# Down projection of a decoder layer by Strassen's seven products

## The chip, the cores and the metric

The kernel runs on one NeuronCore of a Trainium2 chip. The metric is the device time of one execution in microseconds; the profile's times count from the first recorded instruction. The engines are named as in the profile: PE (TensorE, with PEld for its weight loads), DVE (VectorE), ACT (ScalarE), POOL (GpSimd) and SP (SyncE, which here only issues transfers).

## The reference

One decoder layer over 512 tokens of 1024 channels: a mixer (mLSTM heads and a convolution group), and then a feed-forward part of 2816 hidden channels. The change is in the latter:

```python
u = rms_norm(x, ffn_pre_g[l]) * (1.0 + sc2) + sh2
up = causal_dwconv(u @ ffn_up[l], ffn_conv_w[l], ffn_conv_b[l])
a, gt = jnp.split(up, 2, axis=-1)
f = (jax.nn.silu(gt) * a) @ ffn_down[l]
x = x + g2 * rms_norm(f, ffn_post_g[l])
```

All arrays are float32.

## The kernel before, in words

Matmuls run in three passes on rounded values: each operand is split into a high part (a rounded copy by ACT, L182) and a low part (the rest, by a subtraction on POOL or DVE, L183), and `mm3` (L198) adds high x high, high x low and low x high in PSUM. `w_load` (L186) loads up to 2048 columns of weights with one transfer on SP's queue into one of two `raws` buffers and splits them into pieces of 512 columns; a pool of 20 tiles holds the split pieces, so about two and a half loads are ahead of PE.

The up projection goes over 22 blocks i of 128 hidden channels. Block i has a half `a` and a half `gt`, 8 x 3 matmuls each with all 512 tokens as the moving side. ACT and DVE then make the causal convolution of three taps (`conv3`, L967: ACT the bias and the last tap from PSUM, DVE the two others), ACT the SiLU of the gate, DVE the product, and ACT and DVE its high and low part; both stay in SBUF in `slots` (44 tiles of 128x512) for all 22 blocks, in the layout channels x tokens.

The down projection adds up 22 row blocks k into eight PSUM banks, four token tiles of 128 by two halves of 512 output columns. Each bank gets 3 matmuls per row block. The first 18 row blocks go row block by row block over all banks; the last four are gone through one token tile after the other, so that the tail of a tile (multiplication by g2, RMS norm, addition of x, store; L1037 to L1049) runs while PE works on the next.

SP and PE execute in the order of the code. For ACT, DVE and POOL a scheduler orders the instructions when the program is built; on the chip each engine then goes strictly through its list, and an instruction that waits holds all behind it. SP's transfers too are issued in one list.

Of the kernel before, what the change touches and what calls it, by code (L numbers as in the profile page):

```python
# [17 lines left out]
P = 128  # L18
# [36 lines left out]
def decoder_layer(ctx, tc, w_glu0, x, c, adaT, vecs, w_glu, w_qko, w_v0, w_v, w_out, w_up, w_down, out):  # L55
# [32 lines left out]
    def slot(name, dt=F32):  # L88
        return slots.tile([P, T], dt, tag="t", name=name)
# [4 lines left out]
    def atbank(name):  # L94
        return psum.tile([P, T], F32, tag="at", bufs=2, name=name)
# [102 lines left out]
    def mm3(ps, a, b, start, stop):  # L198

        PE.matmul(ps, a[0], b[0], start=start, stop=False)  # L200
        PE.matmul(ps, a[0], b[1], start=False, stop=False)  # L201
        PE.matmul(ps, a[1], b[0], start=False, stop=stop)  # L202
# [772 lines left out]
    f = []  # L975
    for i in range(NF):
        if i < NE:
            pa, pg = early[i]
        else:
            pieces = w_load(w_up[i], f"wup{i}")  # L980
            if i in (4, 8, 12, 16):
                ada_block(38 + i // 2, last_lo[0])
                ada_block(39 + i // 2, last_lo[0])
# [16 lines left out]
        V.tensor_tensor(out=a, in0=a, in1=g, op=ALU.mult)  # L1000
        if i < 2:
            hl = vpool.tile([P, 2 * T + 8], F32R, tag="vh", name=f"fhl{i}")
            hi, lo = hl[:, :T], hl[:, T : 2 * T]
        else:
            hi, lo = slot(f"fh{i}", F32R), slot(f"fl{i}", F32R)
        S.activation(hi, a, AF.Copy)
        V.tensor_tensor(out=lo, in0=a, in1=hi.bitcast(F32), op=ALU.subtract)
        f.append((hi, lo))


    KD = 18
    fsq = const.tile([P, 2 * NT], F32, name="fsq")
    banks = [[atbank(f"dn{tt}_{hf}") if tt == 0 else cvbank(f"dn{tt}_{hf}") if tt == 1 else mmbank(f"dn{tt}_{hf}")
              for hf in range(2)] for tt in range(NT)]
    wd = {}

    def down_rows(k):

        if k % 2 == 0:
            pieces = w_load(w_down[k // 2], f"wd{k}")  # L1020
            wd[k], wd[k + 1] = pieces[:2], pieces[2:]
        return wd[k]

    def down_mm(k, tt):
        for hf in range(2):
            mm3(banks[tt][hf], (f[k][0][:, tok(tt)], f[k][1][:, tok(tt)]), wd[k][hf], k == 0, k == NF - 1)

    for k in range(KD):
        down_rows(k)
        for tt in range(NT):  # L1030
            down_mm(k, tt)
    for k in range(KD, NF):
        down_rows(k)
    for tt in range(NT):
        for k in range(KD, NF):
            down_mm(k, tt)
# [80 lines left out]
```

## Time and profile before

| what | value |
|---|---|
| median of 3 runs | 800.17 us (799.45 to 800.42) |
| span of the profiled execution, first to last instruction | 795.9 us |
| granted clock of TensorE over the span | 0.995 of full speed |
| up projection, first matmul to first matmul of the down projection | 424.7 to 668.3 us |
| down projection, first to last matmul | 668.3 to 788.1 us |
| HBM read, written | 102.08 MB, 4.21 MB |
| weight transfers of 1024 KB in the down projection | 11, landing 4.8 us after issue |

The executions of the runs agree within 0.1%. The profile gives, by engine, the busy time and what ended the idle time before an instruction. The chain of waits follows the last instruction back through what released each step. In the view in order of time, the columns are start, duration, engine, line, operation, tiles and shape.

### The profile page before, as it was taken

How to read it: one execution, taken by the hardware profiler on the slowest of the kernel's cores; microseconds unless marked ns; L12 is line 12 of the kernel's file. 1: busy time of each engine (PE TensorE's matmuls, PEld its weight loads, DVE VectorE, ACT ScalarE, POOL GpSimd, SP SyncE). 2: the span in 40 equal slices, each digit the busy share in tenths (PEclk: the TensorE clock that was granted, in tenths of full speed). 3: DMA queues.
4: the chain of work that ended last, by engine and by line, in shares of the span. 5: the costliest groups of instructions: out<-in, count | busy, mean ns of one | idle time of the engine just before them, and what ended most of it. 6: DMA issues, size and time to landing. Idle time of an engine off the chain costs nothing.

```text
span 795.9 us, 10370 instructions
## 1 busy us (share of the span) xinstructions
PE 781.6 (98%) x3786; PEld 652.2 (82%) x3786; DVE 474.5 (60%) x748; ACT 380.1 (48%) x709; POOL 436.5 (55%) x351
## 2 busy tenths in 40 slices
PE   7999999999999999999999999999999999999996
PEld 5888897777888888888889988888888888888885
DVE  6769999999996435547958794455444453000014
ACT  6684548758474454561345454444444444212212
POOL 4789759869598433442841474444454444444420
PEclk9999999999999999999999999999999999999998
DMA  8963214122037231426854652222222222222205
GB/s 326 347 243 133 81 61 153 54 105 107 28 94 250 80 133 55 159 106 235 320 187 157 218 180 106 106 75 84 106 106 106 105 90 97 107 105 106 80 0 186
DMA packets 24887, 106.97 MB, mean 134 GB/s; under 512 B 2914, under 2 KB 2946, under 8 KB 17412
## 3 DMA queue, kind: packets, MB, share of 16 engines
q1 hardware_dynamic: 16740, 83.22, 29.3%
q10 hardware_dynamic: 8096, 23.08, 8.2%
q8 instruction: 30, 0.49, 0.3%
q14 instruction: 21, 0.17, 0.1%
HBM read 102.08 MB, written 4.21 MB: 134 GB/s over the span
## 4 chain that ended last, share of the span: by engine, by line
PE 90%; DVE 5%; ACT 1%; DMA 1%; issue 1%; DVEq 0%; POOL 0%; SPq 0%; POOLq 0%; ACTq 0%
PE up L201 10%; PE up L200 10%; PE up L202 10%; PE dn L202 5%; PE dn L200 5%; PE dn L201 5%; PE qko L200 4%; PE qko L201 4%; PE qko L202 4%; PE glu L345 4%; DVE cv L716 3%; PE glu L200 2%; PE glu L201 2%; PE glu L202 2%; PE s L514 2%; PE mixa L202 2%
## 5 line engine op out<-in xcount | busy, mean ns | idle before, releaser
L716 DVE SCALAR_TENSOR_TENSOR cv<-gt,cvw,cv 128x502 f32<-128x502 f32 (+24 forms) x200 | 134.4, 725 | 1.9 <-ACT cv L704 1.3
L1043 DVE TENSOR_TENSOR fo<-dn,g2r 128x512 f32<-128x512 f32 x8 | 5.5, 692 | 100.3 <-PE dn L202 100.3
L712 POOL TENSOR_TENSOR cs<-cs,cs 128x510 f32<-128x510 f32 (+3 forms) x32 | 42.8, 1341 | 3.6 <-ACT cs L710 3.6
L183 POOL TENSOR_TENSOR wup_1024l<-wup,wup_1024h 128x512 fp32r<-128x512 f32 x20 | 27.0, 1348 | 31.8 <-ACT wup_1024h L182 31.7
L183 POOL TENSOR_TENSOR wup_1536l<-wup,wup_1536h 128x512 fp32r<-128x512 f32 x20 | 27.0, 1352 | 29.1 <-ACT wup_1536h L182 29.0
L183 POOL TENSOR_TENSOR wup_512l<-wup,wup_512h 128x512 fp32r<-128x512 f32 x20 | 26.8, 1338 | 23.4 <-ACT wup_512h L182 23.4
L183 POOL TENSOR_TENSOR wup_0l<-wup,wup_0h 128x512 fp32r<-128x512 f32 x20 | 27.2, 1358 | 20.8 <-ACT wup_0h L182 20.8
L201 PE MATMUL up<-u2l,wup_0h 128*128 128x512 f32 (+1 forms) x100 | 36.5, 365 | 0.2 <-DVE u2l L885 0.2
L200 PE MATMUL up<-u2h,wup_0h 128*128 128x512 f32 (+1 forms) x100 | 36.5, 365 | 0.0
L200 PE MATMUL up<-u2h,wup_1024h 128*128 128x512 f32 (+1 forms) x100 | 36.4, 364 | 0.0
L202 PE MATMUL up<-u2h,wup_0l 128*128 128x512 f32 (+1 forms) x100 | 36.4, 364 | 0.0
L200 PE MATMUL up<-u2h,wup_512h 128*128 128x512 f32 (+1 forms) x100 | 36.4, 364 | 0.0
L201 PE MATMUL up<-u2l,wup_512h 128*128 128x512 f32 (+1 forms) x100 | 36.4, 364 | 0.0
L202 PE MATMUL up<-u2h,wup_512l 128*128 128x512 f32 (+1 forms) x100 | 36.4, 364 | 0.0
L200 PE MATMUL up<-u2h,wup_1536h 128*128 128x512 f32 (+1 forms) x100 | 36.4, 364 | 0.0
L201 PE MATMUL up<-u2l,wup_1536h 128*128 128x512 f32 (+1 forms) x100 | 36.4, 364 | 0.0
L202 PE MATMUL up<-u2h,wup_1536l 128*128 128x512 f32 (+1 forms) x100 | 36.4, 364 | 0.0
L202 PE MATMUL up<-u2h,wup_1024l 128*128 128x512 f32 (+1 forms) x100 | 36.4, 364 | 0.0
L201 PE MATMUL up<-u2l,wup_1024h 128*128 128x512 f32 (+1 forms) x100 | 36.3, 363 | 0.0
L167 DVE SCALAR_TENSOR_TENSOR junk<-ada,cb 128x1024 bf16<-128x1024 f32 x20 | 32.6, 1631 | 6.3 <-DMA ada<-in_adaT 6.2
L183 POOL TENSOR_TENSOR wqko_1024l<-wqko,wqko_1024h 128x512 fp32r<-128x512 f32 x12 | 16.6, 1380 | 25.8 <-PE v L201 15.1
L183 POOL TENSOR_TENSOR wd_1024l<-wd,wd_1024h 128x512 fp32r<-128x512 f32 x11 | 14.3, 1296 | 29.8 <-ACT wd_1024h L182 29.8
(727 smaller groups left out, 2617.0 us busy)
## 6 DMA issues: line engine op xcount, KB each, us to landing
wup<-in_w_up SPq DMA_DIRECT2D x22, 1024.0 KB, 4.8
wqko<-in_w_qko SPq DMA_DIRECT2D x12, 1024.0 KB, 4.7
wd<-in_w_down SPq DMA_DIRECT2D x11, 1024.0 KB, 4.8
ada<-in_adaT ACTq DMA_DIRECT2D x20, 512.0 KB, 5.6
ada<-in_adaT SPq DMA_DIRECT2D x16, 512.0 KB, 7.6
wo<-in_w_out SPq DMA_DIRECT2D x8, 1024.0 KB, 4.7
spare<-in_adaT ACTq DMA_DIRECT2D x12, 512.0 KB, 8.4
wglu<-in_w_glu SPq DMA_DIRECT2D x5, 1024.0 KB, 8.3
```

The costliest lines, as they stand in the source:

```text
L167: t = V.scalar_tensor_tensor(out=junk, in0=r, scalar=1.0, in1=cb, op0=ALU.mult, op1=ALU.mult, accum_out=mod[:, i : i + 1])
L183: (eng or G).tensor_tensor(out=lo[:, :n], in0=src, in1=hi[:, :n].bitcast(F32), op=ALU.subtract)
L200: PE.matmul(ps, a[0], b[0], start=start, stop=False)
L201: PE.matmul(ps, a[0], b[1], start=False, stop=False)
L202: PE.matmul(ps, a[1], b[0], start=False, stop=stop)
L345: PE.matmul(ps, blk(wk, i)[a], u[k][b], start=k == 0 and p == 0, stop=k == KT - 1 and p == 1)
L514: PE.matmul(sp[:, :n], ks[d][:, cc * P : (cc + 1) * P], qs[d][:, cc * P :], start=d == 0, stop=d == 1)
L712: G.tensor_tensor(out=side[:, d:], in0=side[:, d:], in1=t[:, d:], op=ALU.add)
L716: last_tap = V.scalar_tensor_tensor(out=cp[:, d:], in0=cvx[j][:, : T - d], scalar=w(CK - 1 - d), in1=cp[:, d:], op0=ALU.mult, op1=ALU.add)
L1043: V.tensor_tensor(out=m, in0=banks[tt][hf], in1=g2r[hf], op=ALU.mult)
```

## The change

The hidden channels of the first 18 row blocks are taken as nine pairs, the 512 tokens as two halves, and the 1024 output columns as two halves, so that a pair gives a product of 2x2 blocks: A11, A12 (first token half, even and odd row block), A21, A22 and B11 to B22 (the weights). Strassen's identity in Winograd's form makes the four output blocks from seven products instead of eight:

- left sides: x = (A11, A12); y with A21 + A22 and that minus A11; q with A11 - A21 and A12 minus the second half of y; and A22;
- right sides: B11, B21, B22 as they are, and four sums t1 to t4 of the B's;
- products p1, p2, p6, p5, p7, p3, p4 in this order, each over all nine pairs, 6 matmuls per pair, in one or two of the output blocks' banks. Partial results are copied from PSUM (`keep`, ACT) and added to other banks (`put`, DVE).

The sums of the weights are made during the up projection, at blocks 3, 4, 6, 8, 10, 11, 13, 15 and 17: SP loads four pieces of 256 KB of a pair into `slots`, DVE and POOL make two subtractions each, and SP stores the four sums in DRAM two blocks later. For the activations, POOL makes the four half sums of each pair; x and y are split and stay in SBUF, q and A22 go to DRAM (`spill`) and come back in the down projection (`back`: load, high part by ACT, low part by POOL). The weights of the products come in transfers of three pairs (768 KB) and are split with the low part on DVE and POOL in turn. The last four row blocks are computed as before. Nothing of the result is left out.

The core of the diff:

```diff
-    def mm3(ps, a, b, start, stop):
-
-        PE.matmul(ps, a[0], b[0], start=start, stop=False)
-        PE.matmul(ps, a[0], b[1], start=False, stop=False)
-        PE.matmul(ps, a[1], b[0], start=False, stop=stop)
+    def mm3(ps, a, b, start, stop, again=False):
+
+        for i, (l, r) in enumerate(((a[0], b[0]), (a[0], b[1]), (a[1], b[0]))):
+            PE.matmul(ps, l, r, start=start and i == 0, stop=stop and i == 2, skip_group_check=again)
...
+    JP = 9
+    NP = 2 * JP
+    GJ = 3
+    AT = [NE + 7 * j // 4 for j in range(JP)]
+    spill = {q: dram.tile([P, JP * T], F32, tag=f"spill{q}", name=f"spill{q}") for q in ("t1", "t2", "t3", "t4", "s34", "a22")}
+    sums = {}
+
+    def weight_load(j):
+        sums[j] = [slot(f"b{j}_{q}") for q in range(4)]
+        for q, t in enumerate(sums[j]):
+            nc.sync.dma_start(t, w_down[j][:, q * T : (q + 1) * T])
+
+    def weight_sums(j):
+
+        b11, b12, b21, b22 = sums[j]
+        V.tensor_tensor(out=b11, in0=b12, in1=b11, op=ALU.subtract)
+        G.tensor_tensor(out=b12, in0=b22, in1=b12, op=ALU.subtract)
+        V.tensor_tensor(out=b22, in0=b22, in1=b11, op=ALU.subtract)
+        G.tensor_tensor(out=b21, in0=b21, in1=b22, op=ALU.subtract)
+
+    def weight_store(j):
+        for q, t in zip(("t1", "t3", "t4", "t2"), sums.pop(j)):
+            nc.sync.dma_start(spill[q][:, j * T : (j + 1) * T], t)
...
+            if i in AT:
+                weight_load(AT.index(i))
+            if i - 2 in AT:
+                weight_store(AT.index(i - 2))
+            if i % 2 == 0 and 4 <= i < 4 + NP:
+                j = (i - 4) // 2
+                x_, r_, q_ = rest[j]
+                nc.sync.dma_start(spill["s34"][:, j * T : (j + 1) * T], q_)
+                nc.sync.dma_start(spill["a22"][:, j * HT : (j + 1) * HT], r_[:, HT:])
...
+            if i % 2 == 0:
+                x_, r_ = slot(f"fx{i}"), slot(f"fr{i}")
+            cs = slice(i % 2 * HT, (i % 2 + 1) * HT)
+            V.tensor_tensor(out=x_[:, cs], in0=a[:, :HT], in1=g[:, :HT], op=ALU.mult)
+            V.tensor_tensor(out=r_[:, cs], in0=a[:, HT:], in1=g[:, HT:], op=ALU.mult)
+            if i % 2:
+                y_, q_ = slot(f"fy{i}"), slot(f"fq{i}")
+                G.tensor_tensor(out=y_[:, :HT], in0=r_[:, :HT], in1=r_[:, HT:], op=ALU.add)
+                G.tensor_tensor(out=y_[:, HT:], in0=y_[:, :HT], in1=x_[:, :HT], op=ALU.subtract)
+                G.tensor_tensor(out=q_[:, :HT], in0=x_[:, :HT], in1=r_[:, :HT], op=ALU.subtract)
+                G.tensor_tensor(out=q_[:, HT:], in0=x_[:, HT:], in1=y_[:, HT:], op=ALU.subtract)
+                af.append(split_f(x_, f"fx{i}", i == 1))
+                asum.append(split_f(y_, f"fy{i}", i == 1))
+                rest.append((x_, r_, q_))
+        if i in AT:
+            weight_sums(AT.index(i))
...
+    def product(weights, left, th, hf, start, name):
+
+        for a in range(0, JP, GJ):
+            r = raws.tile([P, 2048], F32, tag="raw", name=f"{name}_{a}")
+            view = weights(a)
+            nc.sync.dma_start(r[:, : GJ * T].rearrange("p (j n) -> p j n", j=GJ), view)
+            for n in range(GJ):
+                j = a + n
+                turn[0] += 1
+                w = w_split(r[:, n * T : (n + 1) * T], f"{name}_{j}", eng=V if turn[0] % 2 else G)
+                hi, lo, off = left(j)
+                for q in range(2):
+                    ts = slice(off + q * P, off + (q + 1) * P)
+                    mm3(banks[2 * th + q][hf], (hi[:, ts], lo[:, ts]), w, start and j == 0, j == JP - 1, True)
+
+    def plain(q):
+        return lambda a: w_down[a : a + GJ, :, q * T : (q + 1) * T].rearrange("j p n -> p j n")
+
+    def summed(q):
+        return lambda a: spill[q][:, a * T : (a + GJ) * T].rearrange("p (j n) -> p j n", j=GJ)
+
+    def keep(th, hf, name):
+        out = [cvtile(f"{name}{q}") for q in range(2)]
+        for q, t in enumerate(out):
+            S.activation(t, banks[2 * th + q][hf], AF.Copy)
+        return out
+
+    def put(kept, th, hf):
...
+    def back(q, a, n, name):
+        t = slot(f"{name}r")
+        nc.sync.dma_start(t[:, :n], spill[q][:, a : a + n])
+        hi, lo = slot(f"{name}h", F32R), slot(f"{name}l", F32R)
+        S.activation(hi[:, :n], t[:, :n], AF.Copy)
+        G.tensor_tensor(out=lo[:, :n], in0=t[:, :n], in1=hi[:, :n].bitcast(F32), op=ALU.subtract)
+        return hi, lo
+
+    product(plain(0), lambda j: (*af[j], 0), 1, 1, True, "p1")
+    p1 = keep(1, 1, "kp1")
+    product(plain(2), lambda j: (*af[j], HT), 0, 0, True, "p2")
+    put(p1, 0, 0)
+    product(summed("t2"), lambda j: (*asum[j], HT), 1, 1, False, "p6")
+    u2 = keep(1, 1, "ku2")
+    s34 = [back("s34", j * T, T, f"s34_{j}") for j in range(JP)]
+    product(summed("t1"), lambda j: (*asum[j], 0), 0, 1, True, "p5")
+    p5 = keep(0, 1, "kp5")
+    product(summed("t3"), lambda j: (*s34[j], 0), 1, 1, False, "p7")
+    u3 = keep(1, 1, "ku3")
+    put(p5, 1, 1)
+    a22 = [back("a22", a * HT, min(T, (JP - a) * HT), f"a22_{a}") for a in range(0, JP, 2)]
+    product(plain(3), lambda j: (*s34[j], HT), 0, 1, False, "p3")
+    put(u2, 0, 1)
+    product(summed("t4"), lambda j: (*a22[j // 2], j % 2 * HT), 1, 0, True, "p4")
+    put(u3, 1, 0)
```

What follows shows how the lists of the engines change. A name like `wup11_512h` is the high part (`l`: the low part) of the piece of `wup11` from column 512 on; `fa10c` and `fg10c` are the two halves of block 10 in the convolution, L970/L969 is its step on ACT, L999/L1043 the SiLU. First ACT's list around block 10, before:

```order
L182 ACTIVATE wup12_1536h_5336<-wup12_5322 128x512
L970 ACTIVATE fa10c_5226<-up10_0_5176,vec_108 128x512
L182 ACTIVATE wup13_0h_5414<-wup13_5412 128x512
L182 ACTIVATE wup13_512h_5418<-wup13_5412 128x512
L970 ACTIVATE fg10c_5230<-up10_1_5201,vec_108 128x512
L182 ACTIVATE wup13_1024h_5422<-wup13_5412 128x512
L999 ACTIVATE fg10c_5230<-fg10c_5230 128x512
L1006 ACTIVATE fh10_5236<-fa10c_5226 128x512
L182 ACTIVATE wup13_1536h_5426<-wup13_5412 128x512
L970 ACTIVATE fa11c_5308<-up11_0_5258,vec_108 128x512
```

And the same place after the change (`fy9` is the sum y of the pair of blocks 8 and 9; L1007 makes its high part):

```order
L1007 ACTIVATE fx9h_5272<-fx8_5179 128x512
L969 ACTIVATE fa10c_5362<-up10_0_5312,vec_108 128x512
L1007 ACTIVATE fy9h_5276<-fy9_5266 128x512
L969 ACTIVATE fg10c_5366<-up10_1_5337,vec_108 128x512
L1043 ACTIVATE fg10c_5366<-fg10c_5366 128x512
L182 ACTIVATE wup11_0h_5381<-wup11_5379 128x512
L182 ACTIVATE wup11_512h_5385<-wup11_5379 128x512
L182 ACTIVATE wup11_1024h_5389<-wup11_5379 128x512
L182 ACTIVATE wup11_1536h_5393<-wup11_5379 128x512
L182 ACTIVATE wup12_0h_5486<-wup12_5484 128x512
```

Between the two steps of block 10 stood the splits of wup13; now no split stands there, and that of wup11 follows behind the SiLU of block 10. POOL's list at this place held only splits, `wup12_1536l`, `wup13_0l` and so on; now it is this (`fy9`, `fq9` are half sums of the pair 8, 9; `b4` are the weights of the fifth pair):

```order
L1055 TENSOR_TENSOR fy9_5266<-fr8_5180 128x256
L1057 TENSOR_TENSOR fq9_5267<-fx8_5179,fr8_5180 128x256
L1056 TENSOR_TENSOR fy9_5266<-fy9_5266,fx8_5179 128x256
L1058 TENSOR_TENSOR fq9_5267<-fx8_5179,fy9_5266 128x256
L990 TENSOR_TENSOR b4_1_5299<-b4_3_5301,b4_1_5299 128x512
L992 TENSOR_TENSOR b4_2_5300<-b4_2_5300,b4_3_5301 128x512
L183 TENSOR_TENSOR wup11_0l_5382<-wup11_5379,wup11_0h_5381 128x512
L183 TENSOR_TENSOR wup11_512l_5386<-wup11_5379,wup11_512h_5385 128x512
```

The low part of wup11 stands behind six operations of the change. Two of them take in what DVE makes here:

```order
L971 SCALAR_TENSOR_TENSOR fa10c_5362<-up10_0_5312,vec_108,fa10c_5362 128x511
L971 SCALAR_TENSOR_TENSOR fa10c_5362<-up10_0_5312,vec_108,fa10c_5362 128x510
L1008 TENSOR_TENSOR fy9l_5277<-fy9_5266,fy9h_5276 128x512
L989 TENSOR_TENSOR b4_0_5298<-b4_1_5299,b4_0_5298 128x512
L971 SCALAR_TENSOR_TENSOR fg10c_5366<-up10_1_5337,vec_108,fg10c_5366 128x511
L971 SCALAR_TENSOR_TENSOR fg10c_5366<-up10_1_5337,vec_108,fg10c_5366 128x510
L991 TENSOR_TENSOR b4_3_5301<-b4_3_5301,b4_0_5298 128x512
```

The sums `b4_0` and `b4_3` stand between and behind the taps of block 10. The last place is ACT at the change from product p6 to p5 in the down projection (`ku2` copies the banks of p6 out of PSUM, `s34` is what was spilled as q):

```order
L1108 ACTIVATE s34_5h_6765<-s34_5r_6763 128x512
L1096 ACTIVATE ku20_6729<-dn2_1_6427 128x512
L1096 ACTIVATE ku21_6730<-dn3_1_6428 128x512
L1108 ACTIVATE s34_6h_6771<-s34_6r_6769 128x512
L1108 ACTIVATE s34_7h_6777<-s34_7r_6775 128x512
L1108 ACTIVATE s34_8h_6783<-s34_8r_6781 128x512
L182 ACTIVATE p5_0h_6789<-p5_0_6787 128x512
```

Before, this list held only splits of weights (`wd4_1024h`, `wd4_1536h`, `wd6_0h` and so on) at that place; now p5's first split follows the two copies. POOL there:

```order
L1109 TENSOR_TENSOR s34_5l_6766<-s34_5r_6763,s34_5h_6765 128x512
L1109 TENSOR_TENSOR s34_6l_6772<-s34_6r_6769,s34_6h_6771 128x512
L1109 TENSOR_TENSOR s34_7l_6778<-s34_7r_6775,s34_7h_6777 128x512
L1109 TENSOR_TENSOR s34_8l_6784<-s34_8r_6781,s34_8h_6783 128x512
L183 TENSOR_TENSOR p5_0l_6790<-p5_0_6787,p5_0h_6789 128x512
```

More of the change, by code (lines that the diff above doesn't have):

```diff
@@ L1013, in decoder_layer @@
-    banks = [[atbank(f"dn{tt}_{hf}") if tt == 0 else cvbank(f"dn{tt}_{hf}") if tt == 1 else mmbank(f"dn{tt}_{hf}")
-              for hf in range(2)] for tt in range(NT)]
-    wd = {}
[L1017 to L1026, printed above, removed]
@@ new lines, in plain @@
+    def plain(q):
[8 more added lines that the diff above has]
+    def put(kept, th, hf):
+        for q, t in enumerate(kept):
+            ps = banks[2 * th + q][hf]
+            V.tensor_tensor(out=ps, in0=ps, in1=t, op=ALU.add)
```

42 lines of the change are left out of this document (24 added, 18 removed).

## Prediction

> **What bounds the kernel now.** I read the page first (busy shares, the 40 slices, the chain of waits), then the windows of the two stages that the change touches, then the order of time inside one block of the up projection.
>
> ```profile
> span 795.9 us, 10370 instructions
> ...
> PE 781.6 (98%) x3786; PEld 652.2 (82%) x3786; DVE 474.5 (60%) x748; ACT 380.1 (48%) x709; POOL 436.5 (55%) x351
> ...
> PE 90%; DVE 5%; ACT 1%; DMA 1%; issue 1%; DVEq 0%; POOL 0%; SPq 0%; POOLq 0%; ACTq 0%
> ...
> 550.00:600.00 50.00, 50.00 (x222) 41.40 (x222) 24.41 (x30) 22.59 (x37) 23.77 (x19) 1.00 0.23 85
> ...
> 700.00:750.00 50.00, 50.00 (x222) 41.44 (x221) 0.00 (x0) 11.76 (x19) 22.95 (x18) 1.00 0.31 115
> ```
>
> TensorE (PE) is busy in all of both windows; the others work less than half of the time (columns: length, then PE, weight loads, DVE, ACT, POOL with counts, clock, DMA share, GB/s). 90% of the chain is PE. So two things count: matmuls taken away, and PE made to wait. The down projection's pace is read from its first and its last matmul:
>
> ```profile
> 668.31 0.39 PE L200 MATMUL dn<-wd_0h,fhl 128*128 128x512 f32 x1
> ...
> 788.13 0.39 PE L202 MATMUL dn<-wd_1536h,fl 128*128 128x512 f32 x1
> ```
>
> 22 row blocks x 4 token tiles x 2 halves x 3 passes are 528 matmuls: 119.82 us / 527 steps = 0.2274 us each. The recorded 0.39 us is a duration in a pipeline, not the pace.
>
> **Matmuls removed.** 18 row blocks took 18 x 24 = 432; seven products of nine pairs take 7 x 9 x 6 = 378. 54 fewer x 0.2274 = **-12.3 us**, on the path.
>
> **What is moved: the splits of the next weights.** This carries the forecast. In order of time, the work that follows one half block of the up projection is:
>
> ```profile
> 559.93 0.76 ACT L970 ACTIVATE fg11c<-up,vec 128x512 f32<-128x512 f32 x1
> ...
> 560.72 1.54 DVE L972 SCALAR_TENSOR_TENSOR fg11c<-up,vec,fg11c 128x511 f32<-128x511 f32 x2 [3.52 <-ACT fg11c L970]
> 562.65 0.61 ACT L999 ACTIVATE fg11c<-fg11c 128x512 f32<-128x512 f32 x1
> ...
> 565.36 0.69 DVE L1007 TENSOR_TENSOR fl<-fa11c,fh 128x512 fp32r<-128x512 f32 x1 [0.70 <-ACT fh L1006]
> ...
> 567.24 0.33 SPq L190 DMA_DIRECT2D wup<-in_w_up  x1
> 567.54 0.63 ACT L182 ACTIVATE wup_0h<-wup 128x512 fp32r<-128x512 f32 x1 [1.02 <-POOL wup_1536l L183]
> 568.25 1.29 POOL L183 TENSOR_TENSOR wup_0l<-wup,wup_0h 128x512 fp32r<-128x512 f32 x1 [1.03 <-ACT wup_0h L182]
> ```
>
> Before, the splits that ACT makes around block 10 are those of block 13. In the changed program ACT stands at wup11's first split only behind the SiLU of block 10's second half. PE cannot begin block 11 before that split, and the SiLU cannot begin before PE has ended block 10. So ACT's order itself makes PE stop. At this boundary PE waits: end of the last matmul's pipeline 0.16 (0.39 - 0.23), bias 0.76, two taps 1.54, SiLU 0.61, split 0.63, and some 0.04 for each of four handovers (559.93 + 0.76 to 560.72 is 0.03): **3.9 us** to the first matmul. The third matmul needs wup11_0l. On POOL that stands behind b4_2, which waits for DVE's b4_3, which stands behind both taps: 0.16 + 0.76 + 1.54 + 0.69 = 3.15, then b4_2 1.29 and wup11_0l 1.29: 5.7, with the DVE's own halves contending 6.3 (below). Two matmuls ran meanwhile (0.45): stall about **5.8 us**. The load is not what is late. SP now issues 36 loads of w_down pieces, 36 stores of sums and 18 spills between the up weights, some 0.33 us each (30 us of SP's time, hidden beside PE); a store that waits for its sums holds the next up load behind it. But the store ahead of wup11 is of sums that block 8 allows, so wup11 is issued while PE is in block 9, and a megabyte lands in 4.8 us:
>
> ```profile
> wd<-in_w_down SPq DMA_DIRECT2D x11, 1024.0 KB, 4.8
> ...
> xr<-x1d SPq DMA_DIRECT2D x8, 256.0 KB, 3.2
> ```
>
> The same order (SiLU of block i-1, then the split of i) stands at blocks 5, 7, 9, 11, 14, 16 and 18: seven stalls. At 14, 16 and 18 the sums are earlier, but POOL does two half operations between wup's first and second low part:
>
> ```profile
> L183 POOL TENSOR_TENSOR wglu_512l<-wglu,wglu_512h 128x256 fp32r<-128x256 f32 x8 | 5.9, 736 | 0.1
> ```
>
> 0.74 x 2 + 1.29 against the 2.7 us that one piece lasts PE: 3.9 + 1.29 - 0.45 + about 1 = 5.8 again. Block 4 splits before the SiLU, but its low part waits behind two sums that wait for a DVE late with the adaT products: I take 8 (bounds 6 and 10). Together 7 x 5.8 + 8 = **+49 us**; bounds 29 (only ACT's legs: 7 x 3.9 + 1.4) and 64 (8 each). Between the stalls PE has two blocks ready and runs dense.
>
> The added work itself fits: per pair of blocks (21.8 us) DVE gets two sums more (1.4 us), POOL two sums and four halves (2 x 1.29 + 4 x 0.74 = 5.5), ACT nothing. But DVE and POOL are not independent:
>
> ```profile
> L1000 DVE TENSOR_TENSOR fa0c<-fa0c,fg0c x1: 685/685/685, 453.6 to 453.6; 128x512 f32<-128x512 f32 x1
> ...
> L1000 DVE TENSOR_TENSOR fa11c<-fa11c,fg11c x1: 1369/1369/1369, 563.3 to 563.3; 128x512 f32<-128x512 f32 x1
> ...
> 562.82 1.30 POOL L183 TENSOR_TENSOR wup_1024l<-wup,wup_1024h 128x512 fp32r<-128x512 f32 x1 [1.43 <-ACT wup_1024h L182]
> ```
>
> The same product of two SBUF tiles takes 0.69 us alone and 1.37 when it meets a POOL operation, ending 0.54 after it. So I add their times where they meet; that is the 0.6 above.
>
> **Clock.** These stalls are long enough to cost more than themselves. At the start of this trace:
>
> ```profile
> 14.00:15.00 1.00, 0.40 (x4) 0.15 (x2) 0.96 (x4) 0.69 (x2) 0.23 (x1) 1.00 1.02 418
> 15.00:16.00 1.00, 0.36 (x3) 0.36 (x4) 0.75 (x2) 0.98 (x2) 1.00 (x1) 1.00 1.02 403
> ...
> 17.50:18.00 0.50, 0.50 (x3) 0.40 (x2) 0.50 (x1) 0.50 (x3) 0.50 (x1) 0.50 1.05 418
> ...
> 20.50:21.00 0.50, 0.50 (x4) 0.41 (x3) 0.50 (x1) 0.49 (x1) 0.00 (x0) 1.00 1.19 295
> ...
> 17.48 0.63 PE L345 MATMUL glu<-uh,wglu_0h 128*128 128x512 f32 x1
> 17.90 0.63 PE L345 MATMUL glu<-uh,wglu_0l 128*128 128x512 f32 x1
> ```
>
> After two microseconds with PE 40% busy the granted clock is 0.50 up to about 20.3, and matmuls go at 0.42 us. 3.4 us at that pace lose 3.4 x (1 - 0.2274/0.42) = 1.6 us; some of it falls into the idle time itself. I take 1.0 for each of eight stalls: **+8** (bounds 0 and 13).
>
> [...]
>
> **The down projection.** Its feed is hidden in steady state: per two blocks of weights PE takes 12 x 0.2274 = 2.73 us, ACT's splits 1.26, and DVE plus POOL one after the other 0.69 + 1.29 = 1.98:
>
> ```profile
> L182 ACT ACTIVATE wd_0h<-wd 128x512 fp32r<-128x512 f32 x11 | 7.0, 632 | 37.1 <-PE dn L201 33.1 <-POOL wd_1536l L183 2.0 <-DVE fa19c L972 1.9
> ...
> L183 POOL TENSOR_TENSOR wd_0l<-wd,wd_0h 128x512 fp32r<-128x512 f32 x11 | 14.3, 1297 | 27.2 <-ACT wd_0h L182 27.2
> ...
> 788.66 0.60 ACT L665 ACTIVATE dn_0junk<-dn 128x512 bf16<-128x512 f32 x1 [4.03 <-DVE fo L1043]
> ```
>
> A load of 768 KB lies between 3.2 and 4.8 us: 4.0 as an estimate. With its splits, 3.3, that is 7.3 for each of two raw buffers, against 8.2 us of PE work: hidden, with little to spare. The copies out of and additions into PSUM go beside the next product (12.3 us, other banks). Three places are not hidden. At the end of p6 ACT holds ku20 and ku21, which wait for PE, ahead of three s34 splits and p5's first: 2 x 0.60 + 4 x 0.63 = 3.7 to the first matmul. POOL's three s34 low parts and p5_0l run from 2.1 us on, 4 x 1.29: 7.3, less 0.45: **6.8**. Before p3, POOL has three and a half a22 low parts ahead of p3_0l, and the feed has lost its lead: **4.5** (0 to 6). The last eight splits come one by one from POOL at 1.29 against three matmuls of 0.68: 8 x 0.61 = **4.9**, where before they lay ready. Sum -12.3 + 16.2 = **+4** (bounds -6 and +23, the latter if every load takes a half longer).
>
> **The sum.** 795.9 + 49 + 8 + 4 = 857 us of span; the runs' median, 800.17, is 4.3 above the span: **861 us**.
>
> **Rivals.** (1) *The saving comes through*: PE has enough split weights in hand when it reaches each block, as in the windows above, and only the 54 matmuls are felt: 800.2 - 12.3 = 788 us. It decides at one point, whether wup11's split is done before PE ends block 10. PE's 50.00 in 50 speaks for it; the place of that split behind block 10's SiLU speaks against. Chance 0.03. (2) *Short stalls*: the low parts catch up behind ACT's legs, the clock holds: 29 + 10 of the 16 below the up projection - 12.3 is +27: 827 us; the free time of POOL (half) speaks for it, its queue order against. 0.12. (3) *Transfers bind*: a pair of blocks moves two megabytes of up weights, one of w_down, one of sums and 0.4 of spills, some 4.6 MB in 21.8 us, 211 GB/s against 85 in the window above. Each landing half as long again makes blocks and products wait for data: the down bound +23 in place of +4, and 1 to 2 us more at eight stalls: 890. The slices near 340 GB/s at the start speak against it, stores between loads for it. 0.15.
>
> ```profile
> GB/s 326 347 243 133 81 61 153 54 105 107 28 94 250 80 133 55 159 106 235 320 187 157 218 180 106 106 75 84 106 106 106 105 90 97 107 105 106 80 0 186
> ```
>
> **Chances.** The forecast has 0.68 (845 to 882 by itself), 0.02 goes to sums that cancel. The range 838 to 886 takes in the forecast's terms and the near side of (2) and (3). Faster by over 0.2% 0.03, within 0.2% 0.02, slower by over 0.2% 0.95; 0.2% is about what a measurement of this kernel can tell from no change.
>
> **What would show it.** PE idle of 5 to 7 us before the first matmuls of blocks 5, 7, 9, 11, 14, 16, 18, put down to ACT wup_0h and then POOL wup_0l; clock below 1 behind them; 474 dn matmuls; one idle of some 7 us at p5. If PE stays dense through the up projection, the reading of ACT's order is wrong; if it waits there for DMA, rival (3) is right.

## The result, and the profile after

| | before | after |
|---|---|---|
| median of 4 runs each, in turn on one chip | 800.29 us (799.45 to 802.26) | 864.97 us (864.18 to 867.5) |
| ratio, with its 95% interval | | 1.0819 (1.0799 to 1.0838) |
| span of the profiled execution | 795.9 us | 865.8 us |
| up projection, first matmul to first of the down projection | 243.6 us | 307.8 us |
| down projection, first to last matmul | 119.8 us | 123.1 us |

The kernel became 8.2% slower; 861 us were forecast. First the page of the kernel after: busy time by engine, the granted clock in 40 slices, and the chain of waits.

```profile
span 865.8 us, 10702 instructions
...
PE 801.4 (93%) x3732; PEld 656.3 (76%) x3732; DVE 526.7 (61%) x824; ACT 403.4 (47%) x758; POOL 499.4 (58%) x414
...
PEclk9999999999999999999999788988989999998999
...
PE 65%; POOL 9%; issue 8%; DVE 8%; DMA 6%; ACT 4%; POOLq 0%; DVEq 0%; ACTq 0%; SPq 0%
...
wup<-in_w_up SPq DMA_DIRECT2D x22, 1024.0 KB, 5.2
```

54 matmuls are gone (3786 to 3732), and yet PE's busy time grew, mainly in the up projection (243.4 to 267.8 us), where matmuls at half clock last longer (0.63 us recorded, 0.39 at full clock). PE's share of the chain fell from 90% to 65%. The clock falls from the 23rd slice on (476 us), where block 4 begins. A weight load lands in 5.2 us where it took 4.8: the loads are hardly slower. The same two windows as before (length, PE, PEld, DVE, ACT, POOL, clock, DMA share, GB/s):

```profile
550.00:600.00 50.00, 40.35 (x154) 31.52 (x153) 24.30 (x28) 17.26 (x30) 30.51 (x27) 0.86 0.37 131
700.00:750.00 50.00, 50.00 (x222) 41.20 (x221) 24.86 (x33) 27.39 (x45) 23.77 (x19) 1.00 0.46 153
```

In the first, where PE did 222 matmuls without a gap, it now does 154 in 40.35 us of busy time, at a clock of 0.86. In the second, with blocks 19 to 21 and the start of the down projection, PE is as dense as before. What PE waited for is in the view of waits of the kernel after (us in total, times, longest):

```profile
PE up L201 <- ACT wup_0h L182: 29.1, 8, 4.2
PE up L201 <- POOL wup_0l L183: 10.7, 8, 5.5
PE dn L201 <- POOL p_0l L183: 5.5, 2, 3.9
...
PE dn L201 <- ACT p_0h L182: 2.8, 1, 2.8
```

Eight stalls for ACT's first split and eight for POOL's first low part, and none for a DMA. The stall ahead of block 11, in order of time in the kernel after (start, duration, engine, line; in brackets the idle time before it and what ended it):

```profile
566.51 0.33 SPq L190 DMA_DIRECT2D wup<-in_w_up  x1
...
586.75 0.39 PE L201 MATMUL up<-u2h,wup_1536l 128*128 128x512 f32 x1
587.17 0.78 ACT L969 ACTIVATE fg10c<-up,vec 128x512 f32<-128x512 f32 x1 [3.69 <-PE up L201]
587.98 1.53 DVE L971 SCALAR_TENSOR_TENSOR fg10c<-up,vec,fg10c 128x511 f32<-128x511 f32 x2 [2.70 <-ACT fg10c L969]
589.43 0.68 DVE L991 TENSOR_TENSOR b<-b,b 128x512 f32<-128x512 f32 x1
589.61 0.63 ACT L1043 ACTIVATE fg10c<-fg10c 128x512 f32<-128x512 f32 x1 [1.66 <-DVE fg10c L971]
590.15 0.61 ACT L182 ACTIVATE wup_0h<-wup 128x512 fp32r<-128x512 f32 x1
590.19 1.27 POOL L992 TENSOR_TENSOR b<-b,b 128x512 f32<-128x512 f32 x1 [3.55 <-DVE b L991]
590.81 0.80 PE L201 MATMUL up<-u2h,wup_0h 128*128 128x512 f32 x1 [3.68 <-ACT wup_0h L182]
591.42 1.45 POOL L183 TENSOR_TENSOR wup_0l<-wup,wup_0h 128x512 fp32r<-128x512 f32 x1
592.93 0.80 PE L201 MATMUL up<-u2h,wup_0l 128*128 128x512 f32 x1 [0.90 <-POOL wup_0l L183]
593.52 0.63 PE L201 MATMUL up<-u2h,wup_0h 128*128 128x512 f32 x1
593.95 0.63 PE L201 MATMUL up<-u2l,wup_0h 128*128 128x512 f32 x1
```

PE ends block 10; only then come ACT's bias, DVE's two taps, ACT's SiLU, and behind the SiLU the split that PE wants. Yet its weights were issued at 566.51 and landed some 5 us later: they lay ready for 18 us, and ACT stood idle for 3.69 us at the bias and 1.66 at the SiLU with the split behind both. POOL's low part stands behind a weight sum that waited 3.55 us for DVE. When PE goes on, matmuls follow each other at 0.43 us instead of 0.227.

From the starts of the matmuls I took for every stage what each step is longer than 0.2274 us: "stalls" are steps over 0.59 us, "slow steps" those of 0.34 to 0.59. In the up projection the stalls come to 44.7 us and the slow steps to 18.8 (before: 0.3 and 0.3), together 62.9 us more, of the 64.2 us that this stage lost. They stand at blocks 4, 5, 7, 9, 11, 14, 16 and 18.

### The profile page after: what moved, and what is told of

It reads as the page before. It is cut to its first block, busy times and chain, and to the rows that moved or that the text cites. A ratio compares the mean times of both kernels' runs of the same rounds, so it can differ in the third digit from the quotient of the medians.

```text
span 865.8 us, 10702 instructions
## 1 busy us (share of the span) xinstructions
PE 801.4 (93%) x3732; PEld 656.3 (76%) x3732; DVE 526.7 (61%) x824; ACT 403.4 (47%) x758; POOL 499.4 (58%) x414
## 4 chain that ended last, share of the span: by engine, by line
PE 65%; POOL 9%; issue 8%; DVE 8%; DMA 6%; ACT 4%; POOLq 0%; DVEq 0%; ACTq 0%; SPq 0%
PE up L201 18%; PE qko L201 12%; PE dn L201 8%; PE glu L201 6%; PE mixa L201 5%; PE mixb L201 5%; DMA ada<-in_adaT 3%; PE v L201 3%; PE s L513 2%; DVE cv L715 2%; PE o L524 1%; PE glu L344 1%; POOL wup_0l L183 1%; DMA p<-spillt 1%; DVE junk L167 1%
## 5 line engine op out<-in xcount | busy, mean ns | idle before, releaser
L201 PE MATMUL up<-u2h,wup_0h 128*128 128x512 f32 (+1 forms) x100 | 43.7, 437 | 29.1 <-ACT wup_0h L182 29.1
L201 PE MATMUL up<-u2h,wup_0l 128*128 128x512 f32 (+1 forms) x100 | 44.6, 446 | 10.7 <-POOL wup_0l L183 10.7
L201 PEld LDWEIGHTS up<-u2h,wup_0h 128*128 128x128 f32 x100 | 22.6, 226 | 35.9 <-ACT wup_0h L182 32.5
L201 PE MATMUL up<-u2l,wup_0h 128*128 128x512 f32 (+1 forms) x100 | 42.6, 426 | 0.2 <-DVE u2l L884 0.2
L1055 POOL TENSOR_TENSOR fy<-fr 128x256 f32<-128x256 f32 x9 | 8.8, 978 | 51.9 <-DVE fr L1052 51.9
L201 PEld LDWEIGHTS up<-u2h,wup_0l 128*128 128x128 f32 x100 | 22.8, 228 | 19.2 <-POOL wup_0l L183 15.2
L167 DVE SCALAR_TENSOR_TENSOR junk<-ada,cb 128x1024 bf16<-128x1024 f32 x20 | 29.2, 1459 | 12.1 <-DMA ada<-in_adaT 12.0
L990 POOL TENSOR_TENSOR b<-b,b 128x512 f32<-128x512 f32 x9 | 11.5, 1282 | 29.1 <-DVE b L989 29.1
L709 ACT ACTIVATE cs<-gt,cvw 128x511 f32<-128x511 f32 (+4 forms) x40 | 27.1, 712 | 1.5 <-POOL cs L711 1.0
(1024 smaller groups left out, 2772.4 us busy)
```

Source lines behind the costliest of these rows:

```text
L167: t = V.scalar_tensor_tensor(out=junk, in0=r, scalar=1.0, in1=cb, op0=ALU.mult, op1=ALU.mult, accum_out=mod[:, i : i + 1])
L201: PE.matmul(ps, l, r, start=start and i == 0, stop=stop and i == 2, skip_group_check=again)
L709: S.activation(t[:, d:], cvx[j][:, : T - d], AF.Copy, scale=w(CK - 1 - d))
L990: G.tensor_tensor(out=b12, in0=b22, in1=b12, op=ALU.subtract)
L1055: G.tensor_tensor(out=y_[:, :HT], in0=r_[:, :HT], in1=r_[:, HT:], op=ALU.add)
```

## The experiments

All runs change the kernel after. Ratios are to the kernel before, in runs on the same chip (its medians there: 800.29 for the kernel after; 799.93 for both lists forced, ACT's list forced, loads ahead and fill; 799.62 for half fill, down projection apart, no sums and together; 798.94 for fetches only and together, not forced).

| run | median us | ratio (95%) | up proj. us | stalls, slow steps there | down proj. us |
|---|---|---|---|---|---|
| after | 864.97 | 1.0819 (1.0799 to 1.0838) | 307.8 | 44.7, 18.8 | 123.1 |
| both lists forced | 806.88 | 1.0092 (1.0064 to 1.0119) | 248.5 | 3.6, 1.5 | 122.0 |
| ACT's list forced | 818.62 | 1.0227 (1.0203 to 1.0251) | 261.6 | 14.0, 3.8 | 122.4 |
| loads ahead | 810.71 | 1.0126 (1.0095 to 1.0157) | 253.3 | 6.4, 3.5 | 122.5 |
| fill | 851.83 | 1.0644 (1.0622 to 1.0667) | 292.4 | (filled), 3.1 | 122.4 |
| half fill | 861.12 | 1.0775 (1.0722 to 1.0827) | 303.1 | (half filled), 13.3 | 122.6 |
| down projection apart | 850.37 | 1.0612 (1.0573 to 1.0651) | 305.5 | 42.4, 19.0 | 107.4 |
| no sums | 804.1 | 1.0062 (1.0042 to 1.0081) | 243.6 | 0.3, 0.3 | 123.1 |
| fetches only | 835.41 | 1.0473 (1.0421 to 1.0525) | 273.1 | 22.2, 7.2 | 122.4 |
| together | 785.74 | 0.9820 (0.9805 to 0.9836) | 243.6 | 0.3, 0.3 | 107.4 |
| together, not forced | 791.69 | 0.9916 (0.9885 to 0.9947) | 247.4 | 3.8, 0.3 | 107.4 |

**1. Are the lists the cause? Both lists forced.** The load and the splits of block i+1 are written ahead of the convolution of block i (SP's and PE's lists stay what they were), and order-only dependencies hold later work behind them:

```diff
+    def behind(t, eng):
+        if held.get(eng) is not None:
+            tc.add_manual_dep(t.ins, held[eng].ins.name, mybir.DependencyInfo(mybir.DependencyClass.NoSync, mybir.DependencyReason.DATA),
+                              reason="program order")
...
-        S.activation(t, ps, AF.Identity, bias=vcol("ffn_conv_b", i), scale=w(2))
+        behind(S.activation(t, ps, AF.Identity, bias=vcol("ffn_conv_b", i), scale=w(2)), S)
...
-        G.tensor_tensor(out=b12, in0=b22, in1=b12, op=ALU.subtract)
+        behind(G.tensor_tensor(out=b12, in0=b22, in1=b12, op=ALU.subtract), G)
...
-                G.tensor_tensor(out=y_[:, :HT], in0=r_[:, :HT], in1=r_[:, HT:], op=ALU.add)
+                behind(G.tensor_tensor(out=y_[:, :HT], in0=r_[:, :HT], in1=r_[:, HT:], op=ALU.add), G)
...
+                held[S] = S.activation(hi, r[:, q * T : (q + 1) * T], AF.Copy)
+                held[G] = G.tensor_tensor(out=lo, in0=r[:, q * T : (q + 1) * T], in1=hi.bitcast(F32), op=ALU.subtract)
```

> The changed kernel with the same list on SP and on PE, the same transfers, sums and splits; only ACT's and POOL's lists are forced: all four splits of up block i+1 stand ahead of the first bias of block i on ACT, and their low parts ahead of POOL's first pair operation and weight sum of block i. Theory (the lists make the stalls, and the stalls pull the clock down): of the 39.8 us of idle time and 17.8 us of slow steps in the up projection some 5 to 10 us stay, at blocks 4 and 5, where the weights of these blocks stand behind the first pieces of w_down on SP; up projection 250 to 258 us in place of 307.8, kernel 808 to 818 us, clock in its windows back to 1.00. Rival (the transfers are late, the lists only show it): PE waits at the same blocks, now put down to the DMA of the weights, and the time stays at 855 to 866 us.

Measured: 806.88 us, a little under what was expected and 58 less than the kernel after, with every transfer, sum and split still there. The window of the run with both lists forced:

```profile
550.00:600.00 50.00, 50.00 (x223) 41.39 (x222) 28.15 (x37) 22.72 (x38) 41.11 (x35) 1.00 0.67 230
```

PE is dense and its clock full, while POOL does a third more (41.1 us against 30.5) and DMA moves 230 GB/s where it moved 131. So neither POOL's work nor the transfers were the limit. The rival that the transfers are late falls.

**2. ACT's list alone.** The same without the two lines on POOL.

> As the run with both lists forced, but ACT's list alone: POOL keeps the freedom to do its pair operations and weight sums ahead of the low parts. Theory: the first leg of every stall (3.68 us, put down to ACT) goes; the second leg (put down to POOL's low parts) stays and grows at the blocks that follow a pair of weight sums, 2 to 3 us at four or five of them, with part of the clock's loss: 818 to 832 us. If POOL's list cost nothing of its own, the time is that of the run with both lists forced, within 3 us; if the transfers were late, 855 to 866 us.

Measured: 818.62 us. No wait for ACT is left but one of 1.3 us at block 4; POOL's low part is late at block 4 (5.46 us) and at three later blocks (2.12, 2.12 and 2.10 us). So POOL's list has a price of its own, 12 us here.

**3. Why the lists came out so. Loads ahead.** The load of block i+1 is issued ahead of the w_down pieces, stores and spills of block i; the scheduler makes the lists anew.

```diff
-            pieces = w_load(w_up[i], f"wup{i}")
+            if i == NE:
+                ahead = w_load(w_up[i], f"wup{i}")
+            pieces = ahead
+            if i + 1 < NF:
+                ahead = w_load(w_up[i + 1], f"wup{i + 1}")
```

> The changed kernel with one thing else: each load of up weights stands one block earlier in the code, ahead of the pieces of w_down, the stores and the spills of its block, so that SP issues it before them; nothing is forced on ACT or POOL, the scheduler makes their lists anew. They come out with the splits of a block one to two blocks ahead of PE nearly everywhere. Theory: the place of the up loads in SP's list is what put the splits late in the lists; up projection 250 to 260 us, kernel 810 to 822 us, a stall or two left near blocks 6 and 10. Rival (transfers bind): moving loads ahead of other loads delays those; stalls move to other blocks and the time stays above 845 us.

Measured: 810.71 us, two stalls left, at blocks 6 and 10. A change of place on SP alone is worth 54 us, though SP itself was never what PE waited for.

**4. No sums, and fetches only.** In the first run the sums with their fetches and stores are left out; in the second the fetches are put back at their old place. In both, p6, p5, p7 and p4 read plain pieces of w_down, so the result is not the layer's; the matmuls are as many.

```diff
             pieces = w_load(w_up[i], f"wup{i}")
-            if i in AT:
-                weight_load(AT.index(i))
-            if i - 2 in AT:
-                weight_store(AT.index(i - 2))
...
-        if i in AT:
-            weight_sums(AT.index(i))
...
-    product(summed("t2"), lambda j: (*asum[j], HT), 1, 1, False, "p6")
+    product(plain(1), lambda j: (*asum[j], HT), 1, 1, False, "p6")
```

> The changed kernel without the weight sums: the pieces of w_down are not fetched, added or stored in the up projection, and p6, p5, p7 and p4 read plain pieces in place of the sums, so the output is not the reference's. The pair sums of the activations, their spills and the seven products stay. The scheduler's lists come out with the splits two to three blocks ahead. Theory (the pieces of w_down ahead of the up weights on SP are what put the splits late): no stall over 1.5 us in the up projection, 244 to 250 us there, clock 1.00; the down projection 119 to 124 us as with the sums; kernel 800 to 809 us. Rival (the pair sums on POOL and DVE are what binds): stalls of some us stay at every second block, over 815 us.

> The run without the weight sums, with the fetches of the w_down pieces put back where the changed kernel has them on SP (ahead of the next up weights): the 36 pieces are loaded in the up projection and not used; no sums, no stores, p6, p5, p7 and p4 read plain pieces, so the output is not the reference's. The only difference to that run is 36 loads on SP, and the scheduler's lists come out late again: splits behind the SiLU of the block before at 5, 7, 9 and 11, a block ahead from 13 on. Theory (the place of the fetches on SP makes the lists late): stalls of some 4 to 5 us at blocks 4, 5, 7, 9 and 11 come back, with the slow steps behind them, none later; 823 to 836 us against 804 without the fetches. Rival (the sums and stores made the lists late): 802 to 808 us.

Measured: without them the up projection takes 243.6 us, as before the change to a tenth, with the pair sums of the activations in it. With the 36 fetches, whose data nobody uses, it takes 273.1: stalls are back at blocks 4, 5, 7, 9 and 11, and none later. The waits of PE in the run with fetches only:

```profile
PE up L201 <- ACT wup_0h L182: 16.9, 5, 3.7
...
PE up L201 <- POOL wup_0l L183: 2.5, 5, 0.7
```

So the fetches alone make ACT's list late; the sums and stores add the later stalls and the longer POOL legs. What is special in the fetches shows on SP's queue. In order of time, the kernel before has nine loads one after the other there (the 83.74 us hold the waits between them, for a buffer of `raws`):

```profile
429.43 83.74 SPq L190 DMA_DIRECT2D wup<-in_w_up  x9
```

In the kernel after, in order of time, two groups of four fetches stand for 13 and 9 us ahead of the loads of block 4 and block 5:

```profile
442.10 13.07 SPq L984 DMA_DIRECT2D b<-in_w_down  x4
458.31 0.33 SPq L190 DMA_DIRECT2D wup<-in_w_up  x1
461.14 8.90 SPq L984 DMA_DIRECT2D b<-in_w_down  x4
...
477.39 0.40 SPq L190 DMA_DIRECT2D wup<-in_w_up  x1
```

Their target tiles come out of `slots`, and a tile has to be free before SP can go on; the view of SP's waits puts those of these two groups down to transfers on ACT's queue (9.4 us to the store of x1d, 21.3 us to six loads of adaT). Later groups take some 2.2 us, but a load needs a `raws` buffer that the late splits free late, so the order keeps itself: block 11's weights were issued at 566.51, when block 9's late splits (from 559.86 on) had let its buffer go. That the scheduler counts the same waits when it makes the lists is argued from this; its reckoning isn't in a trace.

**5. Is the half pace the clock's answer to the stalls? Fill.** Matmuls that nobody reads fill each first leg, so PE is busy while it waits; the real work comes no sooner.

```diff
+    FILL = {4: 12, 5: 18, 7: 16, 9: 16, 11: 16, 14: 16, 16: 16, 18: 16}
...
+            if i in FILL:
+                junk = atbank(f"fill{i}")
+                for _ in range(FILL[i]):
+                    PE.matmul(halves(junk), u2h[:, 0, 0, :P], u2h[:, :, 1, :], start=True, stop=True)
```

> The changed kernel with matmuls added that nobody reads, into a bank of their own, ahead of the up blocks that stall: 12 before block 4, 18 before block 5, 16 (3.64 us at 0.2274) before blocks 7, 9, 11, 14, 16 and 18, as long as the first leg of each stall. The real work comes no sooner. Theory (the half pace after each stall is the clock's answer to PE's idle time): the slow steps behind the stalls go, 14 to 18 us of them, the stalls stay as long as they were, and the kernel takes 847 to 853 us, less than without the added work. Rival (the slow steps are PE waiting for operands, or the clock answers to something else): 863 to 872 us.

Measured: 851.83 us; 126 more matmuls make the kernel 13 us faster. The slow steps fall from 18.8 to 3.1 us, and the up projection gets shorter by about as much, 15.4 us. The window of the run with fill:

```profile
550.00:600.00 50.00, 47.07 (x204) 37.67 (x203) 24.79 (x29) 19.77 (x33) 35.10 (x29) 1.00 0.50 178
```

The clock is 1.00 with some 3 us of idle time left in it (50.00 less 47.07). So the half pace was the clock's.

**6. How much idle time does it take? Half fill.** The same with 6, 9 and 8 matmuls.

> As the run with added matmuls ahead of the up blocks that stall, with half as many: 6, 9 and 8, so that each first leg of 3.7 us becomes 1.8 us of matmuls and 1.9 us of idle time, with the second leg (0.2 to 1.6 us) behind it. If the clock falls only after an idle stretch of about 3.4 us, the slow steps go as they did with the full number: 850 to 853 us. If it answers to the busy share of a few us, as the earlier short stalls of 2.1 us hint, some of the slow steps stay: 855 to 862 us, with 1 to 2 us lost at most stalls.

Measured: 861.12 us, with 13.3 us of slow steps. Ahead of block 9 in the run with half fill, in order of time:

```profile
555.47 1.98 PE L1038 MATMUL fill<-u2h 128*128 128x512 f32 x8
559.31 0.62 PE L201 MATMUL up<-u2h,wup_0h 128*128 128x512 f32 x1 [1.87 <-ACT wup_0h L182]
559.73 0.63 PE L201 MATMUL up<-u2l,wup_0h 128*128 128x512 f32 x1
561.44 0.79 PE L201 MATMUL up<-u2h,wup_0l 128*128 128x512 f32 x1 [1.08 <-POOL wup_0l L183]
```

The longest idle time is 1.87 us, and yet PE is at half pace at once (559.31 to 559.73 is 0.42). So the first of the two readings falls.

**7. The down projection apart.** All low parts go to DVE; the returned pieces are fetched and split beside p6, p5 and p7.

```diff
-                w = w_split(r[:, n * T : (n + 1) * T], f"{name}_{j}", eng=V if turn[0] % 2 else G)
+                w = w_split(r[:, n * T : (n + 1) * T], f"{name}_{j}", eng=V)
...
-        G.tensor_tensor(out=lo[:, :n], in0=t[:, :n], in1=hi[:, :n].bitcast(F32), op=ALU.subtract)
+        V.tensor_tensor(out=lo[:, :n], in0=t[:, :n], in1=hi[:, :n].bitcast(F32), op=ALU.subtract)
...
+            if beside:
+                beside(a // GJ)
...
-    product(summed("t2"), lambda j: (*asum[j], HT), 1, 1, False, "p6")
-    s34 = [back("s34", j * T, T, f"s34_{j}") for j in range(JP)]
-    product(summed("t1"), lambda j: (*asum[j], 0), 0, 1, True, "p5")
-    product(summed("t3"), lambda j: (*s34[j], 0), 1, 1, False, "p7")
-    a22 = [back("a22", a * HT, min(T, (JP - a) * HT), f"a22_{a}") for a in range(0, JP, 2)]
+    product(summed("t2"), lambda j: (*asum[j], HT), 1, 1, False, "p6", lambda a: s34_back(1))
+    product(summed("t1"), lambda j: (*asum[j], 0), 0, 1, True, "p5", lambda a: s34_back(3))
+    product(summed("t3"), lambda j: (*s34[j], 0), 1, 1, False, "p7", lambda a: a22_back(2))
...
-        pieces = w_load(w_down[k // 2], f"wd{k}")
+        r = raws.tile([P, 2048], F32, tag="raw", name=f"wd{k}")
+        nc.sync.dma_start(r, w_down[k // 2])
+        pieces = [w_split(r[:, a : a + T], f"wd{k}_{a}", eng=V) for a in range(0, 2048, T)]
```

> The changed kernel with the up projection as it is; in the down projection every low part is made on DVE (0.69 us alone, where POOL took 1.29), and the s34 and a22 pieces are fetched and split a few at a time beside the products p6, p5 and p7 in place of all at once behind them. Theory (the 123.1 us of the down projection are 107.8 us of matmuls and 15 us of waiting for ACT's and POOL's lists): no idle time over 1 us is left there, the stalls at p5 and p3 and ahead of the last eight splits go, first to last matmul 108 to 111 us, kernel 849 to 854 us. Rival (the raw buffers' loads bind there, 768 KB each at 5.5 us): the waits change their name to DMA, and 117 us or more stay.

Measured: 850.37 us, 14.6 less than the kernel after. The first and the last matmul of the stage in the run with the down projection apart:

```profile
734.22 0.39 PE L201 MATMUL dn<-p_0h,fx 128*128 128x512 f32 x1
...
841.66 0.39 PE L201 MATMUL dn<-wd_1536h,f21l 128*128 128x512 f32 x1
```

107.44 us over 473 steps is 0.2271 each: nothing is left but the matmuls. The 768 KB loads do not bind in this run.

**8. Together.** The load's place of run 3, the forced lists of run 1, the down projection of run 7, and the weight sums begun at block 5:

```diff
-    AT = [NE + 7 * j // 4 for j in range(JP)]
+    AT = [5 + 3 * j // 2 for j in range(JP)]
```

> All of the changed kernel's work with: each up load one block earlier on SP, ahead of the pieces of w_down; ACT's splits of block i+1 ahead of the first bias of block i and POOL's low parts ahead of its pair operations and sums; the weight sums begun at block 5 and done for two pairs in every three blocks; and the down projection of the run on the down projection alone. Theory: PE waits nowhere in either stage, up projection 244 to 247 us, down projection 108 to 110 us, and the 12.3 us of the 54 matmuls come through: 787 to 793 us, faster than the kernel before by 0.9 to 1.6%. Rival (moving the same megabytes in less time brings transfers to the front): waits for DMA appear and the time is 796 us or more.

> The run that put everything together, without the forced lists: the up loads one block earlier on SP, the weight sums from block 5 on, the mended down projection; ACT's and POOL's lists are the scheduler's own. The splits come out one to two blocks ahead, with a low part behind a pair operation or sum at blocks 10, 13, 14 and 17. Theory (the place on SP does most of it, the forced lists the rest): down projection 107.4 us as before, 1 to 8 us of short stalls and slow steps in the up projection, 787 to 794 us. Rival (the lists fall behind on the chip as they did in the changed kernel): over 800 us.

Measured: 785.74 us with the forced lists, 1.8% below the kernel before and 1.3 us under what was expected, and 791.69 without them, with two short stalls. The page of the run with everything together:

```profile
PE 771.1 (98%) x3732; PEld 643.1 (82%) x3732; DVE 561.9 (72%) x877; ACT 403.5 (51%) x758; POOL 438.3 (56%) x361
...
PEclk9999999999999999999999999999999999999998
```

and its windows, the two of before:

```profile
550.00:600.00 50.00, 50.00 (x222) 41.40 (x221) 31.89 (x40) 23.98 (x40) 38.00 (x34) 1.00 0.74 255
700.00:750.00 50.00, 50.00 (x222) 41.33 (x222) 27.40 (x46) 25.39 (x47) 0.00 (x0) 1.00 0.61 206
```

The up projection takes 243.6 us as before the change, the down projection 107.4 instead of 119.8: 12.4 us less, the 54 matmuls. The medians differ by 13.9; the 1.5 us more are in neither stage, and their cause is not shown. Single executions differ by more than that ahead of the up projection (below).

## Why the prediction was right, and where it was off

**The bound and the matmuls taken away.** Right: runs 7 and 8 give back 12.4 us for 54 matmuls where -12.3 was forecast, once nothing else is late.

**The splits of the next weights.** Right in mechanism and place: the stalls are at the eight blocks named, put down to ACT's wup_0h and then POOL's wup_0l, and run 1 shows that the lists make them. The first leg was forecast at 3.9 us; PE is idle for 3.68, and the step is 3.84 over the pace. That the load isn't what is late was right too: 18 us lie between landing and split at block 11. The size was off in the second leg. Block 4 was put at 8 us and took 8.7 in two legs, the other seven at 5.8 and took 4.4 to 5.4. At 7, 9 and 11 POOL's sum and the low part came in the forecast order, with 0.2 us of contention (1.45 for 1.29) where I had put 0.6; at 16 and 18 the half operations stood between wup's first and second low part as forecast, but PE did not wait for the second (0.85 us lost in the second leg instead of 1.9). All stalls together 44.4 us more than before; forecast 49.

**Clock.** The step that failed in size: "I take 1.0 for each of eight stalls" gave 8 us with a bound of 13; the slow steps measured 18.5 us more than before, 2.3 a stall, and the fill gave 15.4 of them back. I had priced 3.4 us of half clock a stall, as long as the clock is 0.50 in the trace of before (16.89 to 20.30 us), and let part of it fall into the idle time. In the kernel after, the granted clock is 0.50 for 10.24 us at block 4, for 3.41 at block 16 and for 6.83 at each of the other six, so the pace is still halved when the work is back: six to thirteen matmuls at 0.427 behind each stall. The rows from 14 to 16 us of the trace of before, with PE busy for 0.40 and 0.36 us of 1.00 ahead of the half clock, were the right thing to go by: in the half fill no idle time ahead of block 9 was longer than 1.87 us, and the matmuls behind it went at 0.42.

**The down projection.** +4 was forecast, +3.3 measured, at the places named, from the kernel after in order of time:

```profile
775.21 0.50 PE L201 MATMUL dn<-p_0h,fy 128*128 128x512 f32 x1 [2.76 <-ACT p_0h L182]
779.58 0.79 PE L201 MATMUL dn<-p_0l,fy 128*128 128x512 f32 x1 [3.88 <-POOL p_0l L183]
...
807.93 0.50 PE L201 MATMUL dn<-p_0l,s_0h 128*128 128x512 f32 x1 [1.58 <-POOL p_0l L183]
...
833.13 0.50 PE L201 MATMUL dn<-wd_0l,f18h 128*128 128x512 f32 x1 [0.26 <-POOL wd_0l L183]
```

In steps over the pace, which are 0.16 to 0.27 us longer than the idle time: p5 2.92 + 4.15 = 7.1 us (forecast 6.8); before p3 1.7 (4.5); the last eight splits 0.44 each, 3.5 (4.9); and 3.2 of steps a little over the pace, 2.1 of them at half pace behind p5, that I had not put into this stage. They come to 15.5, less 12.3 for the matmuls. That +4 is so close is in part luck: the two terms that were too large made up for the one that was left out.

**The sum.** Terms against measured, in the profiled executions: up projection 49 + 8 = 57 against 64.2; down projection +4 against +3.3; 2.4 us more lie outside both stages, where single executions differ (last section). The 4.3 us around the span was no fixed sum: in each run that lists both, time less span is 1.7 to 2.1 us (867.5 less 865.8 here). By that the profiled execution of before, at 795.9 + 1.8, was some 2.5 us under its median, and that of after lies 2.5 above its own: from its span to the median it is -0.8 where 4.3 was added. These 5 us too many hid most of the 7 that the up projection's terms were short. That 861 is so close to 864.97 is luck; the terms are not that close.

**The rivals.** Short stalls at a full clock (827 us): the second legs were shorter indeed, but the clock did not hold. Transfers (890 us): no wait of PE for a DMA in either stage, and run 8 moves 255 GB/s in a window without a stall. The saving came through only in the two runs of experiment 8.

## What to carry to other kernels

Where a scheduler orders some engines and the code orders the queue that feeds them, new transfers ahead of the next weights change the orders even where no transfer is late: read the new lists for the place of each split against the work that waits for PE. Forcing those few orders, or putting the next load ahead of new fetches, took a loss of 8.2% down to 0.9% or 1.3%; both together, with the sums begun later and the down projection's low parts and fetches moved, gave a gain of 1.8% with the same matmuls, transfers and sums. Price a stall of PE with the clock behind it: here 2.3 us for each, with stalls of 4.4 to 8.7 us.

## What was not expected of the hardware

**The same stall may cost the clock or not.** The run with loads ahead and the run together, not forced, each have a stall of 1.39 and 0.62 us with two matmuls between. In order of time, the run with loads ahead:

```profile
547.09 0.50 PE L201 MATMUL up<-u2h,wup_0h 128*128 128x512 f32 x1 [1.39 <-ACT wup_0h L182]
547.42 0.40 PE L201 MATMUL up<-u2l,wup_0h 128*128 128x512 f32 x1
548.44 0.79 PE L201 MATMUL up<-u2h,wup_0l 128*128 128x512 f32 x1 [0.62 <-POOL wup_0l L183]
549.03 0.63 PE L201 MATMUL up<-u2h,wup_0h 128*128 128x512 f32 x1
549.46 0.63 PE L201 MATMUL up<-u2l,wup_0h 128*128 128x512 f32 x1
```

and the run together, not forced:

```profile
542.29 0.50 PE L201 MATMUL up<-u2h,wup_0h 128*128 128x512 f32 x1 [1.39 <-ACT wup_0h L182]
542.63 0.40 PE L201 MATMUL up<-u2l,wup_0h 128*128 128x512 f32 x1
543.64 0.50 PE L201 MATMUL up<-u2h,wup_0l 128*128 128x512 f32 x1 [0.62 <-POOL wup_0l L183]
543.98 0.40 PE L201 MATMUL up<-u2h,wup_0h 128*128 128x512 f32 x1
544.21 0.39 PE L201 MATMUL up<-u2l,wup_0h 128*128 128x512 f32 x1
```

In the first, the matmuls behind it go at 0.43 us for some 3 us; in the second at 0.23 throughout. Likewise, in the run with ACT's list alone, the first of the three stalls of 2.1 us cost 1.6 us of slow steps and the other two nothing. The traces show where the two differ. In each run that has any, all changes of the granted clock within the two stages lie on one grid of 3.413 us: in the kernel after it falls to 0.50 at 480.10, 500.58, 531.30, 562.02, 589.33, 630.29, 661.01 and 688.32 us in the up projection, and these are 6, 9, 9, 8, 12, 9 and 8 times 3.413 us apart. In these traces the grid does not start with a stall (at block 11 PE stands from 587.14 us, and the clock falls at 589.33), and the clock in one stretch of it goes with what PE did in the stretch before. Here are the stretches with the stall (columns as in the windows above), in the run with loads ahead:

```profile
545.04:548.45 3.41, 1.41 (x6) 0.51 (x5) 1.50 (x2) 1.57 (x3) 1.27 (x1) 1.00 0.62 228
```

and in the run together, not forced:

```profile
538.34:541.75 3.41, 2.56 (x12) 1.79 (x10) 0.00 (x0) 0.81 (x2) 0.00 (x0) 1.00 0.58 210
541.75:545.16 3.41, 2.25 (x9) 1.57 (x10) 3.04 (x3) 2.32 (x5) 2.84 (x2) 1.00 0.00 0
```

In the first, the whole stall lies in one stretch, and the next one is at half clock; in the second, the same stall is parted between two, and the clock holds. A limit can be read from the twelve traces. Count for each matmul the last 0.2274 us (its pace) of its recorded time. Of the 1273 stretches at full clock within the two stages, 41 have the half clock behind them: in these, matmuls take up 42% of the stretch or less, in all others 46% or more. So in these traces the limit lies between the two, whether the idle time is in one piece or in several. The busy time of the view does not tell it: far ahead of these stages, the stretch from 128.53 to 131.94 us in the kernel after has PE busy for 2.95 us, but 20 of its 24 matmuls have 4 columns instead of 512, and the clock is 0.50 in the 3.41 us behind it.

**A spread ahead of the stages.** Twelve programs do the same work up to the up projection, and its first matmul starts between 424.72 us (the kernel before) and 428.70 (the run with the down projection apart). A difference of up to 4 us between two single traces there says nothing of a change.
